# The gates of branches a and c of a two-layer encoder, computed first in each layer as seven products of quarters

## The chip, the cores and the metric

The kernel runs on one core of one Trainium2 chip. The metric is the device time in microseconds (us); lower is better. TensorE (PE) does the matrix products, VectorE (DVE) and ScalarE (ACT) the element work, GpSimd (POOL) little. DMAs are issued from the queues of SyncE (SP) and ACT. [...]

## The reference

Two layers over 640 tokens (512 of a prompt, 8 x 16 of samples), 1024 features, all in fp32. Three branches read the same normalised input, and each is scaled by a gate of its own:

```python
u = rms_norm(x, norm1_g)
z = u @ w_in
(xa, ga, mq, mk, mv, mo, mi, mf, aq, ak, av, g_a, g_b, g_c) = split(z)
...
y_a = (h_a * gelu(ga)) @ w_oa            # h_a: conv and linear recurrence (LRU) on xa
y_b = (h_m * sigmoid(mo)) @ w_ob         # h_m: mLSTM on mq, mk, mv, mi, mf, 4 heads
y_c = attention(q_c, k_all, v_all) @ w_oc  # window of 128, 16 heads, sinks
mix = sigmoid(g_a + b0) * y_a + sigmoid(g_b + b1) * y_b + sigmoid(g_c + b2) * y_c
x = x + mix @ w_out
x = x + square(relu(rms_norm(x, norm2_g) @ w_up)) @ w_down
```

Each of g_a, g_b, g_c is a product of 640 x 1024 by 1024 x 1024.

## The kernel before

**Products.** An fp32 product is made of three passes over pairs "hi" and "lo" of a shorter format: hi x hi, lo x hi, hi x lo. Weights come in blocks of 256 columns; the list `jobs` sets their order. For each block `prep` issues two DMAs of 512 KB on SP's queue (`wraw`, 2 buffers); ACT casts the hi part (`parts`, L164), DVE subtracts for the lo part (L166), into `whi` and `wlo` (6 buffers each). `gemm_w` takes a block as 96 matmuls of 128x320 (L293: two halves of columns, 8 steps of 128 rows, three passes, two halves of the tokens) into the two-buffered PSUM tile `acc`. `gemm_x` (L311) makes the transposed form. `strassen_w` (L255) takes a block as seven products of 12 matmuls, 84 in all, on quarter sums of weights (DVE, `wsum`, L186) and of input; before the change only the MLP's up projection uses it, and its `wsum` tiles come from the pool that `sums[0]` names.

**Order of a layer.** Norm of the input (`take_x`, `norm_scale`: the reciprocal root is a chain of small DVE operations, L120 to L125, at whose end the row `rbc` is spread by PE, L392, and copied); LRU; attention; mLSTM; merges; output projection; MLP. Plain products are dropped in between:

- `gate(i)` (L1010) is one block of branch i's gate: 96 matmuls, then per half a DVE multiplication by `rbc` (L1015), a tanh on ACT (L1016) and a store to the memory buffer `gdr[i]`. For branch a (i = 0) the result stays in SBUF (`kept`).
- `branch_a(j)` (L1023) is `gate(0)` followed by a block of `w_oa`, whose evacuation (L1029) multiplies with the kept gate. One stands in the attention, three after it.
- The attention works on 8 pairs of heads. A pair is: scores (L847), DVE maxima, exponentials on ACT (L825, L826), normalisation on DVE (L827 to L830), transposes on PE (L869), copies `pT`, products with the values (L877), and the transposes of the next pair's q (L969, L971), from which ACT and DVE make `qp`. After four pairs a sample group follows (L901, L915, L927, L937).
- The mLSTM works head by head: projections, four chunks and a last one (L672, L679, L682, L686), for which the 8 sample states pass through `cb` (L589 to L599, loads and stores of 256 KB each), the end of the head (`fin`, `num`, L715), transposes (L721).
- The four `gate(2)` stand behind the last head in the program, with the reload of the attention's output (`ydr[1]`) between them; the merges of c and b follow.

**What sets the order on an engine.** The program is written in the order above; a scheduler then orders each engine's list from a model of its own. It moves independent matmuls forward into gaps that its model sees, so a product that stands behind the attention in the program may fill the attention's pauses on PE. Such matmuls are called fillers below.

Of the kernel before, what the change touches and what calls it, by code (L numbers as in the profile page):

```python
# [9 lines left out]
F32 = mybir.dt.float32  # L10
F32R = mybir.dt.float32r
I32 = mybir.dt.int32
AF = mybir.ActivationFunctionType
# [8 lines left out]
NT = SEQ + DB * DS  # L22
# [53 lines left out]
def trunk(ctx: ExitStack, tc: tile.TileContext, I, O):  # L76
# [59 lines left out]
    def act_tile(p=None):  # L136
        return (p or actp).tile([128, 2, NT], F32R, name="at", tag="at")
# [179 lines left out]
    for l in range(depth):  # L317
        win = I["w_in"][l]

        def cols(c, n=256):  # L320
            return (win[:, c:c + n], n)

        seq = [[cols(c + 256 * h) for c in (C_MK, C_MQ, C_MV, C_MO)] for h in range(4)]
        ga = [cols(C_G[0] + 256 * j) for j in range(4)]
        gb = [cols(C_G[1] + 256 * j) for j in range(4)]
        gc = [cols(C_G[2] + 256 * j) for j in range(4)]
        oa, ob, oc, ow = [[(I[nm][l][:, 256 * j:256 * j + 256], 256) for j in range(4)] for nm in ("w_oa", "w_ob", "w_oc", "w_out")]
        for k, j in LRU_ORDER:
# [78 lines left out]
        return cv, cvh  # L407

    cv, cvh = vectors(0)
    xpool = tc.tile_pool(name="xp0", bufs=8)  # L410
    xp = xpool.__enter__()
    with tc.tile_pool(name="ld", bufs=1) as ld:
        xin = ld.tile([128, 5, D], F32, name="xin")
        xss = ld.tile([128, 10], F32, name="xss")
        xpr = I["x_prompt"][0].rearrange("(t p) d -> p t d", p=128)

        def load(h):
            c = slice(512 * h, 512 * h + 512)
            sp.dma_start(xin[:, 0:2, c], xpr[:, 0:2, c])
            sp.dma_start(xin[:, 2:4, c], xpr[:, 2:4, c])  # L420
            sp.dma_start(xin[:, 4, c], I["x_sample"].rearrange("b s d -> (b s) d")[:, c])

        load(0)
        for _ in prep(0, 0):
            pass
        load(1)
        for _ in prep(0, 1):
            pass
        prepared[0] = 1
        sp.dma_start(cs[:, 128:NCST], cst[:, 128:NCST])  # L430
        xs, u = [], []
        for m in range(8):
            x = xp.tile([128, NT], F32, name="x", tag="x")
            ps = ps_small()
            for t in range(4):
                pe.transpose(ps[:, 128 * t:128 * t + 128], xin[:, t, 128 * m:128 * m + 128], ident)
            dve.tensor_copy(x[:, 0:512], ps)
            ps = ps_small()
            pe.transpose(ps[:, 0:128], xin[:, 4, 128 * m:128 * m + 128], ident)
            act.copy(x[:, 512:640], ps[:, 0:128])  # L440
            xs.append(x)
            u.append(act_tile())
            split(u[m], x, cv[:, 8 * V_N1 + m:8 * V_N1 + m + 1])
            if m % 4 == 1:
                h = m // 4
                for t in range(5):
                    xsq = ld.tile([128, 512], F32, name="xsq", tag="xsq", bufs=2)
                    act.activation(xsq, xin[:, t, 512 * h:512 * h + 512], AF.Square, accum_out=xss[:, 5 * h + t:5 * h + t + 1])
        dve.tensor_tensor(vv[:, 0:5], xss[:, 0:5], xss[:, 5:10], ALU.add)


    def mlstm_gates(l, gp, gtp):
# [286 lines left out]
    def attention(l, ap):  # L739
# [206 lines left out]
        for j in range(4):  # L946
# [9 lines left out]
            if j == 0:  # L956
                gate(1)
            if j == 3:
                branch_a(0)
            gemm_x(u, ev_q, 264 if j == 0 else 256)  # L960
            if j == 1:
                gate(1)
# [21 lines left out]
    for l in range(depth):  # L984
# [18 lines left out]
        xpool.__exit__(None, None, None)  # L1003
        if l > 0:
            hdpool.__exit__(None, None, None)

        ngate = [0, 0, 0]
        kept = []

        def gate(i, keep=False):  # L1010
            def evac(m, acc):
                k = ngate[i]
                ngate[i] += 1
                sg = tr.tile([128, NT], F32, name="sg", tag="sg")
                dve.tensor_tensor(halves(sg), acc[:, :, 0:320], halves(rbc), ALU.mult)  # L1015
                act.activation(sg, sg, AF.Tanh, bias=half(V_BG + i, k), scale=0.5)  # L1016
                if keep:
                    kept.append(sg)
                else:
                    act.dma_start(gdr[i][128 * k:128 * k + 128, :], sg)  # L1020
            gemm_w(u, evac)

        def branch_a(j):  # L1023

            gate(0, True)

            def evac(m, acc):
                sg = kept.pop(0)
                dve.scalar_tensor_tensor(halves(sg), halves(sg), 1.0, acc[:, :, 0:320], op0=ALU.add, op1=ALU.mult)  # L1029
                k = 2 * j + m  # L1030
                sp.dma_start(mdr[128 * k:128 * k + 128, :], sg)
            gemm_w(hg, evac)

# [171 lines left out]


        gate(1)
        gate(1)
        with tc.tile_pool(name="at", bufs=1, reuse_waits="tile") as ap:
            attention(l, ap)  # L1210

# [7 lines left out]
        for j in range(1, 4):  # L1219
            branch_a(j)  # L1220
            if j == 1:
                mlstm_gates(l, gp, gtp)
        hgpool.__exit__(None, None, None)


# [14 lines left out]
        xpool = tc.tile_pool(name=f"xp{l + 1}", bufs=8, reuse_waits="tile")  # L1240
# [224 lines left out]
```

## Time and profile before

| what | value |
|---|---|
| time, median of 3 runs | 2901.86 us (2899.88 to 2904.1) |
| profiled execution, its own time | 2899.9 us |
| its span | 2898.1 us |
| mean granted clock of PE | 0.995 |
| PE busy | 2839.4 us (98%) |
| DVE busy | 1853.8 us (64%) |
| ACT busy | 1312.4 us (45%) |
| DMA | 319.5 MB, 110 GB/s over the span |

The profiled execution lies 2 us under the median; 1.8 us of its time are outside the span. "Busy" is the time in which at least one instruction of the engine ran. Matmuls overlap in the records, so a row of n matmuls that follows densely on another costs the distance between starts, which is a little under its stated duration.

### The profile page before, as it was taken

What the parts mean: (1) busy time and instruction counts of PE and PEld (TensorE: products, weight loads), DVE (VectorE), ACT (ScalarE), POOL (GpSimd) and SP (SyncE); (2) the same over time, 40 slices, a digit from 0 to 9 for tenths busy, and PEclk for the clock granted to TensorE, in tenths of its full rate; (3) what the DMA queues carried; (4) which work ended last, traced back from release to release, by engine and by line L of the source; (5) the groups of instructions that cost most, each with busy time, mean ns of one, the idle gap of its engine ahead of it and who ended that gap; (6) DMA issues with size and microseconds to landing.
All of it is one profiled execution on the core that took longest, in us unless ns stands there. A gap on an engine that the chain in (4) does not pass through costs nothing. (4 is left out here: it accounts for less than half of the span.)

```text
span 2898.1 us, 50789 instructions
## 1 busy us (share of the span) xinstructions
PE 2839.4 (98%) x20134; PEld 2799.9 (97%) x20134; DVE 1853.8 (64%) x3758; ACT 1312.4 (45%) x2767; POOL 26.7 (1%) x65
## 2 busy tenths in 40 slices
PE   8999999999999999999999999999999999999999
PEld 8999999999999999999999999999999999999999
DVE  7967566444565677676679676655445646667772
ACT  5764444333442445444357544443444324443452
POOL 0000000000000000000000000000000000000000
PEclk9999999999999999999999999999999999999999
DMA  5242224444573322222322322334445733222222
GB/s 174 65 123 81 76 82 123 120 136 138 158 259 125 104 72 81 81 80 81 113 67 79 116 73 84 96 101 147 131 141 152 264 110 102 74 88 73 80 81 81
DMA packets 276878, 319.53 MB, mean 110 GB/s; under 512 B 26424, under 2 KB 231016, under 8 KB 276608
## 3 DMA queue, kind: packets, MB, share of 16 engines
q1 hardware_dynamic: 267104, 300.03, 33.8%
q10 hardware_dynamic: 9536, 16.26, 1.6%
q8 instruction: 158, 2.59, 0.4%
q14 instruction: 80, 0.66, 0.1%
HBM read 255.76 MB, written 62.04 MB: 110 GB/s over the span
## 5 line engine op out<-in xcount | busy, mean ns | idle before, releaser
L293 PE MATMUL acc<-at,whi 128*128 128x320 f32 x5120 | 818.0, 312 | 6.9 <-ACT at L133 2.8
L293 PEld LDWEIGHTS acc<-at,whi 128*128 128x128 f32 x5120 | 765.3, 189 | 10.2 <-ACT at L133 3.4
L164 ACT CAST whi<-wraw 128x512 fp32r<-128x512 f32 x680 | 406.9, 619 | 512.7 <-PE acc L293 186.9
L166 DVE TENSOR_TENSOR wlo<-wraw,whi 128x512 fp32r<-128x512 f32 x680 | 451.3, 693 | 173.7 <-ACT whi L164 113.5
L311 PE MATMUL acc<-whi,at 128*128 128x256 f32 (+1 forms) x3040 | 408.5, 284 | 16.9 <-DVE qT L626 4.5
L293 PE MATMUL acc<-at,wlo 128*128 128x320 f32 x2560 | 415.6, 310 | 0.0
L311 PEld LDWEIGHTS acc<-whi,at 128*128 128x128 f32 x3040 | 378.2, 188 | 22.1 <-DVE qT L626 5.5
L293 PEld LDWEIGHTS acc<-at,wlo 128*128 128x128 f32 x2560 | 384.1, 188 | 0.7
L255 PE MATMUL acc<-at,whi 128*128 128x320 f32 x1536 | 266.9, 314 | 8.4 <-ACT at L130 5.5
L255 PEld LDWEIGHTS acc<-at,whi 128*128 128x128 f32 x1536 | 236.9, 191 | 14.4 <-ACT at L130 6.1
L311 PE MATMUL acc<-wlo,at 128*128 128x256 f32 (+1 forms) x1520 | 218.6, 282 | 0.2 <-DVE wlo L166 0.2
L311 PEld LDWEIGHTS acc<-wlo,at 128*128 128x128 f32 x1520 | 196.4, 188 | 0.6 <-DVE wlo L166 0.5
L277 PE MATMUL psb<-at,whi 128*128 128x320 f32 x896 | 171.1, 309 | 0.0
L277 PE MATMUL acc<-at,whi 128*128 128x320 f32 x896 | 169.0, 309 | 0.0
L255 PE MATMUL acc<-at,wlo 128*128 128x320 f32 x768 | 143.8, 310 | 0.0
L277 PEld LDWEIGHTS psb<-at,whi 128*128 128x128 f32 x896 | 141.6, 188 | 0.0
L277 PEld LDWEIGHTS acc<-at,whi 128*128 128x128 f32 x896 | 140.9, 188 | 0.0
L164 ACT CAST whi<-wsum 128x512 fp32r<-128x512 f32 x128 | 79.0, 619 | 129.1 <-PE acc L277 93.3
L255 PEld LDWEIGHTS acc<-at,wlo 128*128 128x128 f32 x768 | 121.5, 190 | 0.0
L166 DVE TENSOR_TENSOR wlo<-wsum,whi 128x512 fp32r<-128x512 f32 x128 | 87.8, 689 | 46.9 <-ACT whi L164 45.1
L277 PE MATMUL acc<-at,wlo 128*128 128x320 f32 x448 | 101.8, 308 | 0.0
L277 PE MATMUL psb<-at,wlo 128*128 128x320 f32 x448 | 100.6, 308 | 0.0
(372 smaller groups left out, 3613.1 us busy)
## 6 DMA issues: line engine op xcount, KB each, us to landing
wraw<-in_w_in SPq DMA_DIRECT2D x160, 512.0 KB
wraw<-in_w_up SPq DMA_DIRECT2D x64, 512.0 KB
wraw<-in_w_down SPq DMA_DIRECT2D x64, 512.0 KB
cb<-in_state_mlstm_C SPq DMA_DIRECT2D x64, 256.0 KB
out_C_s<-cb SPq DMA_DIRECT2D x64, 256.0 KB
gdr<-sg ACTq DMA_DIRECT2D x32, 320.0 KB
rl<-ydr SPq DMA_DIRECT2D x32, 320.0 KB
sg<-gdr SPq DMA_DIRECT2D x32, 320.0 KB
```

The source lines that it names most:

```text
L164: act.copy(hi if shape else hi[:, :, :src.shape[-1]], src)
L166: dve.tensor_tensor(lo if shape else lo[:, :, :src.shape[-1]], src, h.bitcast(F32), ALU.subtract)
L255: pe.matmul(bank[nm], ws[i][:, k, :], xs(nm, k)[:, part], start=(first and i == 0 and k == 0 and part == 0), stop=(i == 1 and k == 3), ski ...
L277: pe.matmul(o[s], lhs, hs[k][:, part, 320 * s:320 * s + 320], start=(k == 0 and i == 0 and part == 0), stop=(i == 1 and k == 3))
L293: pe.matmul(acc[:, s, 0:320], lhs, xs[k][:, part, 320 * s:320 * s + 320], start=(i == 0 and k == 0 and part == 0), stop=(i == 1 and k == 7),)
L311: pe.matmul(o, xs[k][:, part, 128 * t:128 * t + 128], wt[:, k % KQ, 0:n], start=(i == 0 and k == 0 and part == 0), stop=(i == 1 and k == 7),)
```

## The change

At the head of each layer, right behind the norm, two blocks of b's gate and then a new function, `strassen_gates`, make all of a's and c's gates: for four i, quarter sums of the scaled input rows i and 4 + i (two ACT copies, four DVE subtractions of 320 columns, two splits), then eight blocks by `strassen_w`, whose evacuations add the products, multiply by `rbc`, take the tanh and store to `gdr`. The LRU stands behind that. `branch_a` makes the `w_oa` product alone and loads its gate from `gdr[0]`. One block of b's gate stays behind the LRU, one in the attention. No gate is left behind the mLSTM.

```diff
+        jobs += [gb[0], gb[1]]
+        jobs += [(a, n, "s") for a, n in ga + gc]
         for k, j in LRU_ORDER:
             jobs.append(cols((C_XA, C_GA)[k] + 256 * j))
-        jobs += [gb[0], gb[1], cols(C_AKV), gb[2]]
+        jobs += [gb[2], cols(C_AKV), gb[3]]
         for j in range(4):
             if j == 3:
-                jobs += [ga[0], oa[0]]
+                jobs.append(oa[1])
             jobs.append(cols(C_AQ - 8, 264) if j == 0 else cols(C_AQ + 256 * j))
             if j == 1:
-                jobs.append(gb[3])
-        for j in range(1, 4):
-            jobs += [ga[j], oa[j]]
+                jobs.append(oa[0])
+        jobs += oa[2:]
         for j in range(4):
             jobs += seq[j]
-        jobs += gc + oc + ob
+        jobs += oc + ob
...
+    def strassen_gates(l, ut, u, xs, vec, half):
+        t12, t34, xg = [], [], {}
+        for i in range(4):
+            for k in (i, 4 + i):
+                xg[k] = ut.tile([128, NT], F32, name="xg", tag="xg", bufs=2)
+                act.activation(xg[k], xs[k], AF.Copy, scale=vec(V_N1, k))
+            a, b = xg[i], xg[4 + i]
+            t = ut.tile([128, NT], F32, name="ut12", tag="ut12", bufs=1)
+            dve.tensor_tensor(t[:, 0:320], a[:, 320:640], a[:, 0:320], ALU.subtract)
+            dve.tensor_tensor(t[:, 320:640], b[:, 320:640], t[:, 0:320], ALU.subtract)
+            t12.append(act_tile(ut))
+            split(t12[i], t)
...
+            def epi(nm, b):
+                if nm == "p1":
+                    kept["p1"] = copy("g1", b["p1"])
...
+                elif nm == "p6":
+                    u2 = copy("g2", b["p6"])
+                    dve.tensor_tensor(sg[0][:, 320:640], u2, b["p3"], ALU.add)
+                    dve.tensor_tensor(sg[0], sg[0], rbc, ALU.mult)
+                    done(0)
...
+        for i, j in [(0, j) for j in range(4)] + [(2, j) for j in range(4)]:
+            product = job(i, j)
...
+        with tc.tile_pool(name="ut", bufs=8, reuse_waits="tile") as ut:
+            sums[0] = ut
+            gate(1)
+            gate(1)
+            strassen_gates(l, ut, u, xs, vec, half)
...
         def branch_a(j):
 
-            gate(0, True)
-
             def evac(m, acc):
-                sg = kept.pop(0)
+                k = 2 * j + m
+                sg = tr.tile([128, NT], F32, name="sg", tag="sg")
+                with tc.issue_after(wlast[0].ins):
+                    sp.dma_start(sg, gdr[0][128 * k:128 * k + 128, :])
                 dve.scalar_tensor_tensor(halves(sg), halves(sg), 1.0, acc[:, :, 0:320], op0=ALU.add, op1=ALU.mult)
...
         yc = []
-        for j, n in enumerate((4, 0, 3, 0)):
-            yc += reload(ydr[1], hdp, range(len(yc), len(yc) + n))
-            gate(2)
-        yc += reload(ydr[1], hdp, range(7, 8))
+        yc += reload(ydr[1], hdp)
```

**PE in the second half of the attention.** Before, one pair of layer 0 (from its first scores) reads on PE's list; L293 are the fillers, L847, L869 and L877 the pair itself:

```order
L847 MATMUL psb<-kh_2338,qp_2362 128x192 x12
L293 MATMUL acc<-at,whi 128x320 x13
L293 MATMUL acc<-at,wlo 128x320 x16
L293 MATMUL acc<-at,whi 128x320 x14
L869 MATMUL psb<-cs,prob_2368 128x128 x2
L293 MATMUL acc<-at,whi 128x320
L869 MATMUL psb<-cs,prob_2369 128x128 x4
L293 MATMUL acc<-at,whi 128x320 x11
L869 MATMUL psb<-cs,prob_2370 128x128 x4
```

In the changed program the same pair reads as follows (the lines have moved: L920 are the scores, L942 the transposes, L950 the products with the values, L1042 and L1044 the next pair's q):

```order
L920 MATMUL psb<-kh_3684,qp_3708 128x192 x12
L942 MATMUL psb<-cs,prob_3714 128x128 x2
L942 MATMUL psb<-cs,prob_3715 128x128 x4
L950 MATMUL psb<-pT,vd 128x256
L942 MATMUL psb<-cs,prob_3716 128x128 x4
L942 MATMUL psb<-cs,prob_3717 128x128 x4
L950 MATMUL psb<-pT,vd 128x256 x2
L1042 MATMUL psb<-cs,q 128x128 x4
L950 MATMUL psb<-pT,vd 128x256 x4
L1044 MATMUL psb<-cs,q 128x128
L920 MATMUL psb<-kh_3684,qp_3707 128x64 x2
```

No filler is left: from the scores of pair 4 to the end of the second sample group PE's list holds 424 L293 and 48 L311 of other products before, and none of either in the changed program, in each of the two layers. All four `w_oa` blocks stand ahead of pair 4 there.

**PE in the last mLSTM head.** Before, from one chunk's last product to the next chunk (L293 are blocks of c's gate):

```order
L686 MATMUL psb<-vt,kw 128x257 x2
L672 MATMUL psb<-qT,kT 128x128 x2
L293 MATMUL acc<-at,whi 128x320 x22
L293 MATMUL acc<-at,wlo 128x320 x2
L679 MATMUL psb<-vt,pt 128x257
```

Changed (L759, L745, L752 and L755 are these same lines, moved):

```order
L759 MATMUL psb<-vt,kw 128x257 x2
L745 MATMUL psb<-qT,kT 128x128 x2
L752 MATMUL psb<-vt,pt 128x257
L755 MATMUL psb<-cp,qs 128x257 x2
L759 MATMUL psb<-vt,kw 128x257 x2
```

From the first chunk's product L679 (now L752) to the small transposes at the end of the mLSTM (L729, L734; now L802, L807) the list held 337 L293; 32 are left, and those belong to the first block of `w_oc`. Heads 0 to 2 and the attention's first half keep as many fillers as before, give or take a block.

**DVE at the head of layer 1.** The piece of the changed list that leads to the first evacuation of a product (L1086, b's gate); L461 to L467 are subtractions of quarter sums, L131 their splits, L186 sums of weights, L123 to L125 the reciprocal root:

```order
L131 TENSOR_TENSOR at<-ut_16711,at 128x640
L166 TENSOR_TENSOR wlo<-wsum,whi 128x512
L186 TENSOR_TENSOR wsum<-wraw,wsum 128x512
L124 SCALAR_TENSOR_TENSOR tt<-tt,vv 128x5
L131 TENSOR_TENSOR at<-ut_16717,at 128x640
L461 TENSOR_TENSOR ut_16727<-xg 128x320
L186 TENSOR_TENSOR wsum<-wraw 128x512
L125 SCALAR_TENSOR_TENSOR rtok<-tt,rtok 128x5
```

Before, the same steps of the root stand among small operations of the LRU and splits of weights:

```order
L123 TENSOR_TENSOR tt<-rtok 128x5
L1076 SCALAR_TENSOR_TENSOR sm<-sm 128x8
L166 TENSOR_TENSOR wlo<-wraw,whi 128x2x256
L1135 TENSOR_TENSOR lwl<-lwr,lwh 128x256
L124 SCALAR_TENSOR_TENSOR tt<-tt,vv 128x5
L166 TENSOR_TENSOR wlo<-wraw,whi 128x2x256
L1076 SCALAR_TENSOR_TENSOR sm<-sm 128x8
L125 SCALAR_TENSOR_TENSOR rtok<-tt,rtok 128x5
```

All four i of the quarter sums stand ahead of the first evacuation in layer 1 (16 subtractions and 8 splits), in layer 0 two and a half of the four.

## Rows read from the trace of the kernel before

**Rows 1.** The page, engines: busy us (share), instructions.
```profile
PE 2839.4 (98%) x20134; PEld 2799.9 (97%) x20134; DVE 1853.8 (64%) x3758; ACT 1312.4 (45%) x2767; POOL 26.7 (1%) x65
```

**Rows 2.** Windows, layer 0: stretch, length, busy (instructions) per engine, PEclk, DMA.
```profile
850.00:900.00 50.00, 50.00 (x343) 50.00 (x342) 27.44 (x39) 13.17 (x21) 0.00 (x0) 1.00 0.66 230
1050.00:1100.00 50.00, 50.00 (x344) 50.00 (x343) 35.46 (x60) 21.69 (x38) 0.00 (x0) 1.00 0.25 75
```

**Rows 3.** Groups by line and shape, DVE: count | busy us, mean ns | idle before.
```profile
L166 DVE TENSOR_TENSOR wlo<-wraw,whi 128x512 fp32r<-128x512 f32 x672 | 446.1, 693 | 168.7 <-ACT whi L164 113.5 <-PE acc L293 24.3 <-PE acc L255 8.1
L131 DVE TENSOR_TENSOR at<-rl,at 128x640 fp32r<-128x640 f32 x32 | 25.8, 823 | 27.1 <-ACT at L130 27.0
L1386 DVE TENSOR_TENSOR dn<-acc,rbc 128x320 f32<-128x320 f32 x112 | 49.5, 484 | 45.6 <-PE acc L277 45.5
L186 DVE TENSOR_TENSOR wsum<-wraw 128x512 f32<-128x512 f32 x64 | 44.2, 691 | 25.2 <-DMA wraw<-in_w_up 24.5
```

**Rows 4.** Windows of two stretches of layer 0, all engines.
```profile
370.00:471.50 101.50, 101.28 (x724) 98.96 (x723) 64.76 (x140) 44.89 (x139) 6.67 (x11) 1.00 0.30 92
772.30:844.60 72.30, 72.30 (x492) 71.15 (x491) 41.15 (x101) 29.39 (x63) 0.00 (x0) 1.00 0.54 174
```

**Rows 5.** The same two stretches, PE and PEld of L293 alone, then L311.
```profile
370.00:471.50 101.50, 68.31 (x409) 60.67 (x407) 1.00 0.30 92
772.30:844.60 72.30, 59.84 (x378) 55.73 (x377) 1.00 0.54 174
...
370.00:471.50 101.50, 6.06 (x48) 5.82 (x48) 1.00 0.30 92
```

**Rows 6.** Timeline, PE: scores of pairs 5 and 6 (start us, us, engine, line).
```profile
397.18 1.93 PE L847 MATMUL psb<-kh,qp 128*128 128x64 f32 x16
416.69 1.93 PE L847 MATMUL psb<-kh,qp 128*128 128x64 f32 x16
```

**Rows 7.** Timeline, DVE and ACT, within pair 5.
```profile
404.36 1.03 DVE L830 TENSOR_TENSOR prob<-prob,ssm 128x384 f32<-128x384 f32 x2
...
411.11 0.59 ACT L975 ACTIVATE qp<-psb 64x512 fp32r<-64x512 f32 x1 [2.14 <-PE psb L969]
...
413.38 0.69 DVE L976 SCALAR_TENSOR_TENSOR qp<-psb,qp 64x512 fp32r<-64x512 f32 x1 [0.24 <-ACT qp L975]
```

**Rows 8.** Timeline, PE: the second sample group, from its last scores to its end.
```profile
458.36 1.14 PE L915 MATMUL psb<-kcT,qsm 128*128 128x144 f32 x8
464.57 1.03 PE L927 MATMUL psb<-cs,sprob 128*128 128x128 f32 x8
471.41 0.39 PE L937 MATMUL psb<-pT,vn 128*128 128x128 f32 x2
```

**Rows 9.** Timeline, PE and DVE: chunks, sample states and end of head 3.
```profile
777.62 0.59 PE L679 MATMUL psb<-vt,pt 128*128 128x257 f32 x2
795.89 0.59 PE L679 MATMUL psb<-vt,pt 128*128 128x257 f32 x2
...
780.65 0.28 DVE L675 TENSOR_TENSOR pt<-psb,dmat 128x128 f32<-128x128 f32 x1
822.04 0.15 DVE L699 TENSOR_TENSOR den<-csum,psb 128x1 f32<-128x1 f32 x1
829.50 2.07 DVE L715 SCALAR_TENSOR_TENSOR num<-num,fin,mo 128x256 f32<-128x256 f32 x5
```

**Rows 10.** Timeline, PE, layer 0 near 1016 us: around a pause in the Strassen products.
```profile
1016.24 0.63 PE L255 MATMUL acc<-at,whi 128*128 128x320 f32 x1 [2.80 <-ACT at L130]
1021.68 4.41 PE L255 MATMUL acc<-at,whi 128*128 128x320 f32 x16
1026.52 1.33 PE L255 MATMUL acc<-at,whi 128*128 128x320 f32 x8
```

**Rows 11.** A window behind that pause: columns as in Rows 2.
```profile
1020.00:1024.00 4.00, 4.00 (x16) 3.96 (x17) 3.27 (x16) 1.04 (x2) 0.00 (x0) 0.50 0.00 0
```

**Rows 12.** Timeline, PE: the head of layer 1.
```profile
1473.22 6.40 PE L293 MATMUL acc<-at,whi 128*128 128x320 f32 x32 [1.61 <-DVE xq L1106]
```

More of the change, by code (lines that the diff above doesn't have):

```diff
@@ L409, in trunk @@
     cv, cvh = vectors(0)
-    xpool = tc.tile_pool(name="xp0", bufs=8)
+    xpool = tc.tile_pool(name="xp0", bufs=8, side="right")
     xp = xpool.__enter__()
@@ L449, in trunk, with operand, job, copy @@
         dve.tensor_tensor(vv[:, 0:5], xss[:, 0:5], xss[:, 5:10], ALU.add)
+    def strassen_gates(l, ut, u, xs, vec, half):
[10 more added lines that the diff above has]
+            split(t12[i], t)
+            t_ = ut.tile([128, NT], F32, name="ut34", tag="ut34", bufs=1)
+            dve.tensor_tensor(t_[:, 0:320], b[:, 320:640], a[:, 320:640], ALU.subtract)
+            dve.tensor_tensor(t_[:, 320:640], b[:, 0:320], t[:, 320:640], ALU.subtract)
+            t34.append(act_tile(ut))
+            split(t34[i], t_)
+        def operand(nm, i):
+            t, c = {"p1": (u[i], 0), "p2": (u[4 + i], 0), "p3": (u[4 + i], 1),
+                    "p5": (t12[i], 0), "p6": (t12[i], 1), "p7": (t34[i], 0), "p4": (t34[i], 1)}[nm]
+            return t[:, :, 320 * c:320 * c + 320]
+        def job(i, j):
+            sg, kept = {}, {}
+            def copy(nm, src):
+                t = ut.tile([128, 320], F32, name=nm, tag=nm, bufs=2 if nm == "g5" else 1)
+                act.copy(t, src)
+                return t
+            def done(c):
+                k = 2 * j + c
+                act.activation(sg[c], sg[c], AF.Tanh, bias=half(V_BG + i, k), scale=0.5)
+                act.dma_start(gdr[i][128 * k:128 * k + 128, :], sg[c])
+            def epi(nm, b):
+                if nm == "p1":
+                    kept["p1"] = copy("g1", b["p1"])
+                elif nm == "p5":
+                    kept["p5"] = copy("g5", b["p5"])
+                elif nm == "p2":
+                    sg[0] = tr.tile([128, NT], F32, name="sg", tag="sg")
+                    dve.tensor_tensor(sg[0][:, 0:320], kept["p1"], b["p2"], ALU.add)
+                elif nm == "p6":
[3 more added lines that the diff above has]
+                    done(0)
+                elif nm == "p7":
+                    sg[1] = tr.tile([128, NT], F32, name="sg", tag="sg")
+                    dve.tensor_tensor(sg[1][:, 320:640], kept["p5"], b["p7"], ALU.add)
+                    dve.tensor_tensor(sg[1][:, 320:640], sg[1][:, 320:640], rbc[:, 320:640], ALU.mult)
+                elif nm == "p4":
+                    dve.tensor_tensor(sg[1][:, 0:320], b["p4"], rbc[:, 0:320], ALU.mult)
+                    done(1)
+            return strassen_w(operand, epi)
+        before = None
+        for i, j in [(0, j) for j in range(4)] + [(2, j) for j in range(4)]:
+            product = job(i, j)
+            for nm in ("p1", "p5", "q7", "p2", "p3", "q4", "p6"):
+                if nm[0] == "p":
+                    product(nm)
+                elif before is not None:
+                    before("p" + nm[1])
+            before = product
+        before("p7")
+        before("p4")
@@ L958, in attention @@
             if j == 3:
-                branch_a(0)
+                branch_a(1)
             gemm_x(u, ev_q, 264 if j == 0 else 256)
             if j == 1:
-                gate(1)
+                branch_a(0)
             qv = q.rearrange("p t (h d) -> p t h d", d=64)
@@ L1007, in trunk, with gate @@
         ngate = [0, 0, 0]
-        kept = []
-        def gate(i, keep=False):
+        def gate(i):
             def evac(m, acc):
@@ L1207, in trunk @@
         gate(1)
-        gate(1)
         with tc.tile_pool(name="at", bufs=1, reuse_waits="tile") as ap:
@@ L1218, in trunk @@
         gtp = gtpool.__enter__()
[L1219 to L1222, printed above, removed]
+        branch_a(2)
+        mlstm_gates(l, gp, gtp)
+        branch_a(3)
         hgpool.__exit__(None, None, None)
@@ L1232, in trunk @@
         yc = []
-        for j, n in enumerate((4, 0, 3, 0)):
-            yc += reload(ydr[1], hdp, range(len(yc), len(yc) + n))
-            gate(2)
-        yc += reload(ydr[1], hdp, range(7, 8))
+        yc += reload(ydr[1], hdp)
         mix = []
-        xpool = tc.tile_pool(name=f"xp{l + 1}", bufs=8, reuse_waits="tile")
+        xpool = tc.tile_pool(name=f"xp{l + 1}", bufs=8, reuse_waits="tile", side="right")
         xp = xpool.__enter__() if l < depth - 1 else ctx.enter_context(xpool)
```

8 lines of the change are left out of this document (2 added, 6 removed).

## The prediction

> **What bounds the kernel now.** I read the page's engine part first: PE is busy 98% of the span, DVE 64%, ACT 45% [rows 1]. The reader is to see that almost no time is left in which PE waits, so what a change is worth is either matmuls taken away or new waits on PE. The windows by stage give the price of a matmul: 342 of 128x320 in 50 us of plain products [rows 2], 146.2 ns each; the MLP's Strassen stage runs at the same pace (344 in 50 us) although DVE is busy 35 of the 50 us there. Then I looked at what keeps PE full in the stages that have chains of their own, and there the windows say something else than the page: in the attention's second half [rows 4] 409 of 724 matmuls are L293 and 48 are L311 [rows 5], products that have nothing to do with the attention. The last mLSTM head is the same, 378 of 492. Those two stretches are bound by PE only because of the fillers; under them lie chains through ACT and DVE.
>
> **The products that go.** A plain block is 96 matmuls, a Strassen block 84. Sixteen blocks change (a and c, four each, two layers): 192 matmuls x 146.2 ns = **-28.1 us**.
>
> **The Strassen stage itself.** DVE per block: 7 `wlo` and 4 `wsum` at 0.69, three additions and two multiplications on 320 columns at 0.48, one on 640 at 0.82 (by the row of the same width) [rows 3]: 7.6 + 2.4 + 0.8 = 10.8 us, against 84 x 146.2 ns = 12.3 us of PE. It fits, as it does in the MLP [rows 2]. I take nothing; if DVE paced it with some waits in between, a tenth of 12.3 us per block would be 20 us in all.
>
> **Gates through memory.** The sixteen stores and reloads of 320 KB per branch and layer lie beside products, and ACT and the queues have room (DMA share 0.25 to 0.66 of the engines in dense stages [rows 2]). The reload in `branch_a` stands on SP's queue behind the last weight load, and its reader is an evacuation that comes a block later. Nothing; if each of the 16 evacuations waited a us, 16 us.
>
> **The fillers that go.** The order of the changed program shows the second half of the attention without any filler, and the last head with 32. Apart from the 28.1 us the matmuls have not vanished; they are done earlier, at the head of the layer, where they cover nothing. What matters is how long the two stretches take when bare.
>
> *Attention, pairs 4 to 7 and sample group.* The fillers are 409 x 0.146 + 6 = 65.7 us of the 101.5 us, so the stretch's own PE work is 35.8 us [rows 4, 5]. A pair takes 19.5 us now [rows 6]. Its bare chain, from pair 5: scores at 397.18 to the end of normalisation at 405.39 [rows 6, 7]; an evacuation of another product stands in between on DVE, 0.8 by a row of its width [rows 3], so 7.2 with its wait. Then transposes and products 1.0 each (estimated by the scores' 1.93 for 16 matmuls), a copy `pT` 0.7 (as L976, which copies as much [rows 7]), and the two rounds of ACT and DVE for the next q, 411.11 to 414.07 [rows 7], 3.0: **12.9 us**. Sample group and last pair without the next q: 10 for the pair, 3.8 to the end of the scores, 5.1 from there to L927 and 7.1 for the rest [rows 8]: 26. Bare stretch 3 x 12.9 + 26 = 64.7 us, so PE would be idle 64.7 - 35.8 = **29 us** that it now spends on fillers.
>
> *Last head.* Own PE work: 72.3 - 378 x 0.146 = 17.0 us [rows 4, 5]; with the 32 `w_oc` matmuls that stay, 21.7. Bare chain: a chunk from L679 to the next `pt`, 777.62 to 780.93 [rows 9], 3.3 us, four of them 13.2 where it was 18.3 us for three; the sample states took 795.89 to 822.04, 26 us [rows 9]: bare, I choose 20, since two states are in work at a time (some 3 us each, estimated by six operations of 0.5 to 0.7, as the rows of such widths [rows 3]), which bounds it at 12 from below, and loads and stores through five buffers hold it up; the root and scale 822.04 to 829.50, 7.5, of which weight splits take a part, 5; `num` 2.1; the last block of the attention's output, whose buffer comes free only then, 5 for load and split. Sum 45.3, idle **24 us**.
>
> **The clock.** The granted clock is 0.995 in the mean, but it falls where PE pauses: after an idle time of 2.80 us at 1016 [rows 10] 16 matmuls took 4.41 us where 8 took 1.33 at full clock, and the window 1020 to 1024 shows 0.50 with PE busy all the time [rows 11]. [...] In a bare pair PE pauses some 5 us in the softmax (7.2 less the scores' 1.93), and works about half of the time; so I expect 0.5 over most of both stretches. The chain then grows by PE's own parts: per pair 3 us (half of the scores, transposes, products), so 15.9, tail 33, stretch 80.7, lost time **45 us**. Last head: four chunks at 5.2, states 23, rest as before: 55, lost **33 us**. And PE is back at full pace only in the row at 1026.52, 10 us behind the pause [rows 10], so each stretch leaves up to 3 us behind it; I take 2, four times, 8 us. [...]
>
> **Head of a layer.** Both `acc` buffers are full when the first evacuation needs `rbc`, so PE waits for DVE's root; it does already (1.61 us of idle at the end [rows 12]). In layer 1 eight subtractions (0.4 effective), four splits (0.74), four weight sums and one split (0.6) now stand within the root, less an estimated 4.5 us of splits and small operations that stood there before and go: +4.7. Before the root 8.3 us of such work delay the sum of squares, of which 4 us fall in DVE's slack: +4. So +9; layer 0 about +4. Sum **+13 us**; bounds 3 and 25.
>
> **Sum.** -28.1 + 2 x (45 + 33) + 8 + 13 = +149 on the execution's own 2899.9 us, which lies 2 us under the median: **3048 us**. Chance 0.55, own range 3005 to 3090.
>
> **Rivals.** *The clock stays full* in the stretches, because scores, transposes and products come often enough: -28.1 + 2 x (29 + 24) + 13 = +91, 2991 us. For it: PE still works some 55% of a bare stretch (35.8 of 64.7 us), and the one fall above [rows 10] came behind a pause in which it did nothing at all. Chance 0.2.
>
> *The stretches hardly shorten*, because other things than PE's fillers set the pace (buffers of PSUM, the loads of sample states, the order of DVE): then all fillers are lost, 65.7 and 50.6 us per layer, +217, 3117 us. Against it: the parts of a pair's chain add up to 12.9 us from their rows, against a period of 19.5 [rows 6]. With half of the shortening, about 3080. Chance 0.15.
>
> *DVE or the weight sums pace the Strassen stage*: +20 on top of any case. Chance 0.02 that it is the main cause.
>
> *Faster: the fillers covered nothing*, since the chain contracts to PE's own work when it is not interrupted. Then -28.1 + 13: 2885 us. It decides where the four bare stretches leave less than 4 us idle each. Against it: four softmaxes of some 5 us, in which PE has nothing of its own, are already 20 us of idle in one layer's attention. Chance 0.06.
>
> *No change*: gain and idle balance at those 4 us. Chance 0.02.
>
> **Range and signs.** Between 2975 and 3100 lie the likeliest case, the one with full clock and part of the slower one, and about 2 in 10 is left out. About 0.2% (6 us) can be told from no change here. Faster 0.06, same 0.02, slower 0.92.
>
> **What would show it.** In the changed profile: L255 with 1344 more matmuls and L293 with 1536 fewer; PE's idle time up from some 60 us (span less busy [rows 1]) to over 150, ended by ACT and DVE at L942, L950, L920 in the attention and at L666, L670 and L794 in the mLSTM; the distance between the scores of pairs 4 to 7 about 16 us instead of 19.5, and the stretch some 80 us instead of 101; in the windows of these stretches PEclk near 0.5; the Strassen stage at the layer's head with 340 matmuls per 50 us; the first gate evacuation of layer 1 some 9 us later against the norm. The clock is wrong if PEclk is 1.00 in pairs 4 to 7; the whole forecast is wrong if these pairs come 10 us apart or less.

## The result and the profile after

The changed kernel takes 3059.5 us (median of 4 runs, 3055.12 to 3059.93) against 2901.68 us before: a ratio of 1.0538 (95% interval 1.0525 to 1.0551), 5.4% slower. The forecast was 3048 us with 2975 to 3100 as its range.

The page of the changed kernel, engines and the clock by slices of the span (compare [rows 1]):

```profile
PE 2867.7 (94%) x19942; PEld 2809.7 (92%) x19942; DVE 1980.3 (65%) x3982; ACT 1381.2 (45%) x2895; POOL 26.8 (1%) x65
...
PEclk9999998899989999999989999989999899999999
```

PE has 192 instructions fewer and yet is busy 28 us longer and idle 189 us of a span of 3057.1 us, against 59 us before. Longer busy with fewer matmuls is already a sign of the clock, which is 0.967 in the mean against 0.995 before: four of its dips stand where the fillers are gone, one at the head of layer 1. In the kernel before, PE's longest wait in total for one line was this (us in total, times, longest):

```profile
PE acc L255 <- ACT at L130: 5.5, 2, 2.8
```

The six longest in the changed kernel:

```profile
PE psb L942 <- DVE prob L903: 34.4, 9, 7.7
PE acc L311 <- ACT vd L853: 17.3, 2, 8.7
PE psb L794 <- DVE num L788: 17.0, 5, 7.3
PE psb L393 <- DVE rtok L125: 12.8, 2, 11.9
PE psb L920 <- DVE qp L1049: 10.5, 7, 1.7
PE psb L666 <- ACT ch L662: 9.8, 9, 2.3
```

L942 and L920 are the attention, L794 and L666 the mLSTM (13.9 of the 17.0 us at L794 in the last heads), L393 the head of the layer: the places that the forecast named. L311 waiting for `vd` is not among them. It is the product behind the keys and values, between LRU and attention.

The same stages, by the first matmul of each in the timelines of both kernels (us, layer 0 / layer 1):

| from, to | before | after | difference, both layers |
|---|---|---|---|
| end of the layer ahead to first LRU product | 61.1 / 475.1 | 193.6 / 613.6 | +270.9 |
| LRU | 90.6 / 90.5 | 90.5 / 90.6 | 0 |
| LRU to pair 0 | 93.6 / 93.7 | 93.7 / 94.2 | +0.6 |
| pair 0 to pair 4 | 124.8 / 124.8 | 118.8 / 118.9 | -11.9 |
| pair 4 to the end of the sample group | 101.4 / 101.4 | 75.6 / 75.7 | -51.5 |
| from there to the last head's first chunk | 301.0 / 298.8 | 298.9 / 301.8 | +0.9 |
| last head to the small transposes | 66.2 / 66.2 | 46.2 / 47.0 | -39.2 |
| merges to the second norm | 189.3 / 189.8 | 184.2 / 183.9 | -11.0 |

(The first row of layer 1 contains the MLP of layer 0.) The head of the layers got 2 x 126.3 us of products (192 L293 and 672 L255 each at 0.146) and 18 us of waiting. Everywhere else 960 L293 a layer are gone, the 768 of a's and c's gates and the 192 of the two blocks of b that now stand at the head: 281 us in all. Those stages became only 112 us shorter: 169 us, six tenths of the work taken out, had covered waits. By place, with the L293 counted in the traces of both kernels (per layer, layer 0):

| stretch | fillers gone, us | shorter by, us | had covered, us |
|---|---|---|---|
| LRU to pair 0 | 96 L293: 14.0 | -0.1 | 14 |
| pair 0 to pair 4 | 73 L293 less 48 L311 that came: 5 | 5.9 | 0 |
| pair 4 to the end of the sample group | 407 L293 and 48 L311: 65.2 | 25.8 | 39.4 |
| last head | 308 L293: 45.0 | 20.0 | 25.0 |
| merges | 74 L293: 10.8 | 5.1 | 5.7 |

(An L293 is taken at 0.1462 us, an L311 at 0.118, since 24 of them took 2.84 us from 317.66 us on in the changed kernel. On PE's list I had counted 424 L293 in the third stretch; the trace has 407.)

The two bare stretches as windows (answers to [rows 4]; stretch, length, busy per engine with instructions, PEclk, DMA):

```profile
496.61:572.22 75.61, 48.39 (x267) 42.17 (x267) 48.91 (x119) 30.31 (x117) 6.60 (x11) 0.75 0.07 22
871.15:917.35 46.20, 30.52 (x142) 24.76 (x141) 30.74 (x82) 19.71 (x49) 0.00 (x0) 0.74 0.48 151
```

The mean of 0.75 is made of 37.57 us near 0.50 and the rest of the stretch at 1.00. In the timeline of pairs 4 to 6 (answers to [rows 6, 7]) it shows as matmuls of two lengths:

```profile
506.32 1.56 PE L942 MATMUL psb<-cs,prob 128*128 128x128 f32 x6 [7.69 <-DVE prob L903]
...
515.76 2.01 PE L920 MATMUL psb<-kh,qp 128*128 128x64 f32 x16 [1.72 <-DVE qp L1049]
521.04 1.55 PE L942 MATMUL psb<-cs,prob 128*128 128x128 f32 x6 [3.27 <-DVE prob L903]
...
523.24 1.85 PE L942 MATMUL psb<-cs,prob 128*128 128x128 f32 x8
...
529.95 2.08 PE L920 MATMUL psb<-kh,qp 128*128 128x64 f32 x16 [1.72 <-DVE qp L1049]
```

The scores of pair 5 took 2.01 us for 16 at a clock of 1.00, the eight transposes behind the pause 1.85 us at 0.55 in the mean. Eight of them took 1.03 us in pair 5 before, at 1.00:

```profile
407.69 1.03 PE L869 MATMUL psb<-cs,prob 128*128 128x128 f32 x8
```

Pair 5 is 14.2 us long, pair 6 13.9: 12.9 was the bare estimate, 15.9 the one with half the clock. Pair 4 took 19.2 us. PE waits 7.69 us there, because DVE works on another block of q (L841 to L845, 499.82 to 505.76) ahead of the pair's normalisation.

How much the clock can have cost is bounded by the windows in which it was low. There are five in this stretch, each at 0.50 or 0.51, and one in the last head (the first of the five, their sum, the last head's):

```profile
501.00:511.25 10.25, 4.93 (x19) 4.31 (x20) 8.57 (x16) 2.63 (x11) 0.95 (x1) 0.50 0.13 30
...
sum 37.57, PE 22.50 PEld 19.43 DVE 25.05 ACT 16.82 POOL 0.95; mean PE 4.50 PEld 3.89 DVE 5.01 ACT 3.36 POOL 0.19
...
893.54:917.35 23.81, 12.49 (x39) 9.08 (x40) 18.12 (x51) 9.31 (x23) 0.00 (x0) 0.50 0.52 164
```

PE was busy 22.50 us near 0.50 in the attention and 12.49 us in the last head. From the 0.50, and from eight transposes that took 1.91 us at it (pair 4) and 1.03 at 1.00, I estimate that this work would take about half at the full clock, so that the clock cost at most 11 of the 39.4 us lost there, and at most 6 of the 25. The rest, 28 and 19 us or more, is pauses.

### The profile page after: what moved, and what is told of

Same layout as the page of the kernel before. It is cut to its first block, busy times and chain, and to the rows that moved or that the text cites. A ratio compares the mean times of both kernels' runs of the same rounds, so it can differ in the third digit from the quotient of the medians.

```text
span 3057.1 us, 50989 instructions
## 1 busy us (share of the span) xinstructions
PE 2867.7 (94%) x19942; PEld 2809.7 (92%) x19942; DVE 1980.3 (65%) x3982; ACT 1381.2 (45%) x2895; POOL 26.8 (1%) x65
## 4 chain that ended last, share of the span: by engine, by line
PE 81%; DVE 7%; DMA 6%; ACT 4%; issue 2%; SPq 0%; POOL 0%; ACTq 0%; DVEq 0%; POOLq 0%
PE acc L293 24%; PE acc L255 16%; PE acc L311 15%; PE acc L277 6%; PE psb L277 6%; PE psb L255 3%; DMA out_C_s<-cb 2%; PE psb L950 2%; DMA cb<-in_state_mlstm_C 1%; PE psb L942 1%; DVE wlo L166 1%; DMA rl<-ydr 1%; PE psb L759 1%; PE psb L1223 1%; PE psb L755 1%
## 5 line engine op out<-in xcount | busy, mean ns | idle before, releaser
L293 PE MATMUL acc<-at,whi 128*128 128x320 f32 x4096 | 654.5, 314 | 19.6 <-DVE sg L1130 9.6
L164 ACT CAST whi<-wraw 128x512 fp32r<-128x512 f32 (+1 forms) x664 | 398.3, 620 | 559.7 <-PE acc L293 207.7
L293 PEld LDWEIGHTS acc<-at,whi 128*128 128x128 f32 x4096 | 617.8, 191 | 22.9 <-issue 15.4
L166 DVE TENSOR_TENSOR wlo<-wraw,whi 128x512 fp32r<-128x512 f32 (+1 forms) x664 | 439.3, 686 | 200.4 <-ACT whi L164 142.6
L311 PE MATMUL acc<-whi,at 128*128 128x256 f32 (+1 forms) x3040 | 417.5, 287 | 36.1 <-ACT vd L853 17.3
L311 PEld LDWEIGHTS acc<-whi,at 128*128 128x128 f32 x3040 | 385.3, 191 | 42.5 <-ACT vd L853 17.9
L255 PE MATMUL acc<-at,whi 128*128 128x320 f32 x2304 | 392.1, 311 | 9.3 <-ACT at L130 6.4
L255 PEld LDWEIGHTS acc<-at,whi 128*128 128x128 f32 x2304 | 350.8, 189 | 15.6 <-ACT at L130 6.9
L293 PE MATMUL acc<-at,wlo 128*128 128x320 f32 x2048 | 326.5, 309 | 0.0
L293 PEld LDWEIGHTS acc<-at,wlo 128*128 128x128 f32 x2048 | 306.1, 188 | 0.0
L311 PE MATMUL acc<-wlo,at 128*128 128x256 f32 (+1 forms) x1520 | 218.8, 283 | 0.0
L255 PE MATMUL acc<-at,wlo 128*128 128x320 f32 x1152 | 214.9, 309 | 0.0
L164 ACT CAST whi<-wsum 128x512 fp32r<-128x512 f32 x192 | 118.8, 620 | 181.1 <-PE acc L277 93.3
L311 PEld LDWEIGHTS acc<-wlo,at 128*128 128x128 f32 x1520 | 197.9, 190 | 0.1
L255 PEld LDWEIGHTS acc<-at,wlo 128*128 128x128 f32 x1152 | 181.1, 189 | 0.0
L166 DVE TENSOR_TENSOR wlo<-wsum,whi 128x512 fp32r<-128x512 f32 x192 | 131.5, 688 | 59.1 <-ACT whi L164 56.4
L277 PE MATMUL acc<-at,whi 128*128 128x320 f32 x896 | 168.7, 309 | 0.0
L277 PEld LDWEIGHTS acc<-at,whi 128*128 128x128 f32 x896 | 140.8, 188 | 0.0
L277 PE MATMUL acc<-at,wlo 128*128 128x320 f32 x448 | 101.8, 308 | 0.0
```

The lines of the kernel that those rows point to most:

```text
L164: act.copy(hi if shape else hi[:, :, :src.shape[-1]], src)
L166: dve.tensor_tensor(lo if shape else lo[:, :, :src.shape[-1]], src, h.bitcast(F32), ALU.subtract)
L255: pe.matmul(bank[nm], ws[i][:, k, :], xs(nm, k)[:, part], start=(first and i == 0 and k == 0 and part == 0), stop=(i == 1 and k == 3), ski ...
L277: pe.matmul(o[s], lhs, hs[k][:, part, 320 * s:320 * s + 320], start=(k == 0 and i == 0 and part == 0), stop=(i == 1 and k == 3))
L293: pe.matmul(acc[:, s, 0:320], lhs, xs[k][:, part, 320 * s:320 * s + 320], start=(i == 0 and k == 0 and part == 0), stop=(i == 1 and k == 7),)
L311: pe.matmul(o, xs[k][:, part, 128 * t:128 * t + 128], wt[:, k % KQ, 0:n], start=(i == 0 and k == 0 and part == 0), stop=(i == 1 and k == 7),)
```

## The experiments

Two theories were set against each other. **Lost cover**: the plain gates had filled waits of PE, and the new place at the head of the layer has nothing to fill. **A cost of the new stage**: DVE, the weight sums or the trips through memory make each Strassen block dear, wherever the plain ones had been.

**Strassen or place.** The same places with plain products, no quarter sums:

```diff
-        jobs += [(a, n, "s") for a, n in ga + gc]
+        jobs += ga + gc
...
-            strassen_gates(l, ut, u, xs, vec, half)
+            for i in (0, 2):
+                for j in range(4):
+                    gate(i)
```

> The same places and the same trips through memory, but a's and c's gates are plain products (96 matmuls a block instead of 84) and there are no quarter sums. Theory (the place costs the time, the Strassen form itself saves): 28 us more for the matmuls less 12 to 18 us for the quicker head of a layer: 3070 to 3076 us, attention and last head as in the changed kernel. Rival (the Strassen stage costs more than it saves, by DVE or weight sums): 3059 us or less.

Measured 3072.05 us (ratio to before 1.0581, 1.0555 to 1.0607), in the expected window, and its stretches are 76.0 and 46.7 us long in layer 0, as bare as in the changed kernel. By the stages the two heads are 11.3 us longer: 28.1 us more of products, less 16.8 of the 18 us of waiting. So the Strassen form does save; the place costs. The Strassen products themselves run as densely as plain ones, as this window of the changed kernel shows:

```profile
50.00:100.00 50.00, 50.00 (x344) 50.00 (x343) 39.44 (x68) 26.14 (x47) 0.00 (x0) 1.00 0.39 113
```

**Memory.** The kernel before, with a's gates stored and loaded back:

```diff
-            gate(0, True)
+            gate(0)
...
-                sg = kept.pop(0)
+                sg = tr.tile([128, NT], F32, name="sg", tag="sg")
+                with tc.issue_after(wlast[0].ins):
+                    sp.dma_start(sg, gdr[0][128 * k:128 * k + 128, :])
```

> The kernel before with one part of the change alone: the gates of a are stored to memory and loaded back where they are used, instead of being kept in SBUF; all products plain and in their old places. Theory (memory is hidden): 2902 us within 5. Rival (the trip through memory holds up evacuations, 1 us each or more): 2910 us or more.

Measured 2901.62 us, ratio 0.9997 (0.9988 to 1.0006): the trip through memory is hidden.

**Each half back.** c's gates behind the last head again, or a's into the attention again, the other four blocks staying at the head (the edit for c, in part):

```diff
-        jobs += [(a, n, "s") for a, n in ga + gc]
+        jobs += [(a, n, "s") for a, n in ga]
...
-        jobs += oc + ob
+        jobs += gc + oc + ob
...
+            gate(2)
```

> The gates of c go back behind the last mLSTM head as plain products; only a's four blocks per layer stay in the Strassen stage at the head of the layer. Theory (lost cover): the last head was idle about 25 us per layer without fillers, and the four blocks lose 7.0 us of saving: 3059.5 - 49 + 14 = about 3024 us, with the stretch from the head's first chunk to its end back at 66 us and PEclk 1.00 there; the attention's second half stays at 76 us. Rival (the Strassen stage itself, its DVE work and its trips through memory cost the time, so much a block): half the blocks, half the loss, about 2980 us.

> The mirror image: a's gates go back into the attention and behind it as plain products kept in SBUF; c's four blocks stay at the head as Strassen products. Theory (lost cover): the attention's second half was idle or slow for about 40 us per layer, so 3059.5 - 80 + 14 = about 2993 us, the stretch back at 101 us with PEclk 1.00, the last head still at 46 us; where the additional block also covers the wait for the keys and values ahead of the attention (8.7 us per layer) up to 25 us less. Rival (a cost per Strassen block): the same time as with c back, about 2980 us.

Measured 3012.92 us for c back (1.0381, 1.0351 to 1.0411) and 3005.71 us for a back (1.0357, 1.0326 to 1.0387). Neither is near the rival's 2980, but each is some 12 us off the theory's forecast, and they lie closer together than I expected. By the stages of layer 0: with c back the head of the layer is 48.6 us shorter (four blocks of 12.3), the last head 21.0 longer and the merges 5.3. 56.1 us of plain products thus cost 26.3: they cover **30 us** a layer, more than the 25 of the expectation, which had not counted the merges. With a back, 56.1 us of products cost about 22 us: they cover **34 us**, fewer than the 40. The second half of the attention was not full again in that run:

```profile
453.35:547.27 93.92, 87.75 (x602) 83.65 (x600) 59.55 (x132) 39.25 (x132) 6.60 (x11) 0.96 0.27 85
```

It holds 285 L293 there, before it was 407; the rest of a's products stand in the first half.

**Work moved to where cover is missing.** Two of b's plain blocks go behind the last head, one from the head of the layer and one from the start of the attention; the work stays the same:

> Both a and c stay Strassen products at the head; two of b's plain gate blocks (one from the head, one from the start of the attention) move behind the last mLSTM head, where they can fill it. The work is the same, only the place changes. Theory (lost cover): the last head's 25 us per layer are filled, 3059.5 - 49 = about 3010 us; up to 28 us more if the block taken from the start of the attention is missed there. Rival (Strassen stage, DVE or memory cost the time): no change, 3055 to 3065 us.

Measured 3061.77 us: nothing gained, a clear miss. The last head's window in this run (layer 0):

```profile
854.33:921.36 67.03, 54.20 (x332) 51.68 (x331) 38.12 (x94) 28.21 (x61) 0.00 (x0) 0.87 0.53 167
```

67.0 us is as long as with all four blocks of c back (67.2 us with 451 matmuls), with 332 matmuls and pauses in it. The timelines tell where fillers cover and where they don't (layer 0, us, with the number of L293 in brackets; "two behind" is this run, "held" the next one):

| part of the last head | before | changed | two behind | held |
|---|---|---|---|---|
| chunks (first to last L752) | 23.5 (95) | 13.5 (8) | 23.5 (95) | 13.0 (0) |
| sample states (to the last L666 or L670) | 27.3 (145) | 21.0 (16) | 29.9 (119) | 29.1 (143) |
| end of the head, transposes | 15.4 (96) | 11.7 (4) | 13.7 (4) | 15.6 (86) |

Between the chunks 87 fillers more, 12.7 us, cost 10.0: the scheduler has put 24 behind each chunk, while the chunk's chain leaves PE well under a microsecond, as the changed kernel shows:

```profile
873.59 0.70 PE L752 MATMUL psb<-vt,pt 128*128 128x257 f32 x2 [0.53 <-DVE pt L748]
877.16 0.67 PE L752 MATMUL psb<-vt,pt 128*128 128x257 f32 x2 [0.69 <-DVE pt L748]
```

They delay the chain by four fifths of their length. In the sample states of the kernel before, 129 fillers more, 18.9 us, cost 6.3. I had read them as nearly free (22.5 us with them), because I took the last L593, at 818.35 us, for the end; the last product with a state was L597, 4.9 us later (the second row is of the run with two blocks behind):

```profile
823.21 0.29 PE L597 MATMUL psb<-kvs 128*128 128x258 f32 x1
907.05 1.01 PE L670 MATMUL psb<-kvs 128*128 128x258 f32 x4
```

Taking them as nearly free, I held the two blocks behind the first product with a sample state:

```diff
             yc += reload(ydr[1], hdp, range(len(yc), len(yc) + n))
-            gate(1)
+            with tc.issue_after(smark[0].ins):
+                gate(1)
```

> As the run with two of b's gate blocks behind the last head, but these two blocks are ordered behind the first product with a sample state, so that none can stand between the chunks. Theory (a filler costs nothing only where the stage's own chain is waiting; between chunks 94 of them cost 10 us, in the sample states they were nearly free): the last head takes about 50 us instead of 67, 3061.8 - 34 = about 3028 us. Rival (fillers delay the sample states and the end of the head just as much): 3052 to 3062 us.

Measured 3046.29 us (1.0492, 1.0469 to 1.0515), 15 us less than the run before it: the direction is that of lost cover, the size less than half. The last head took 57.7 and 56.0 us instead of 67.0 and 68.8. The chunks were bare again, at 13.0 us, but the sample states stayed at 29.1, far from the 21.0 that "nearly free" had meant. The merges took 6 us more: 3.4 of them are 23 matmuls of `w_oc` that no longer stood in the head, and the rest stays open.

**Fillers held back in the attention.** Three `w_oa` blocks ordered behind the scores of pairs 4, 5 and 6:

```diff
-        branch_a(2)
-        mlstm_gates(l, gp, gtp)
-        branch_a(3)
+        for j in (1, 2, 3):
+            with tc.issue_after(marks[HOLDAT[j - 1]].ins):
+                branch_a(j)
...
```

> As the changed kernel, but three of the four w_oa blocks are ordered behind the scores of pairs 4, 5 and 6, so that the scheduler can't use them up earlier: 288 fillers (42 us) in the attention's second half, as many fewer in its first. Theory (lost cover): the second half takes about 80 us instead of 76 and its clock stays at 1.00, the first half gets shorter by up to 42 us as far as its own chain lets it: 2985 to 3025 us. Rival (the first half starves instead): nothing gained, 3055 to 3065 us, with PE idle between pairs 0 and 4.

Measured 3058.17 us: the rival. The windows of layer 0, pair 0 to 4 and pair 4 to the end:

```profile
379.20:478.05 98.85, 74.38 (x538) 69.47 (x537) 67.42 (x154) 44.34 (x144) 1.91 (x2) 0.90 0.19 62
478.05:571.49 93.44, 89.66 (x603) 86.42 (x603) 59.81 (x137) 37.56 (x129) 6.61 (x11) 0.94 0.29 95
```

48 us of products (288 L293, 48 L311) went from the first half to the second. The first half gave up 20 us, the second took 18. The first had not been over-full: without these blocks PE is idle there for 24 us and the clock falls to 0.90. The whole attention is short of products, and moving those that are left did not mend it.

**The clock.** Useless short matmuls in the pause of the softmax, 48 a pair:

```diff
+                if pair >= 4 and H == 1:
+                    for i in range(48):
+                        pe.matmul(pss[i % 2][:, 192:256], q[:, i % 8].rearrange("p a d -> p (a d)"), kh[g][:, 0, 0:64],
+                                  start=True, stop=True)
```

> As the changed kernel, with 48 extra matmuls of 64 columns in each of pairs 4 to 7, whose results are used nowhere: 17 stand ahead of the last four scores, 29 in PE's pause of the softmax, 2 behind the first transposes. They add about 3 us of work a pair in the pause and nothing useful. Theory (the pause drops the clock to half, and the pair's transposes and products then take twice as long): PEclk 0.9 or more in pairs 5 to 7, eight transposes 1.0 us instead of 1.9, the pairs 12.5 to 13.2 us apart instead of 14.0, the total down by 4 to 10 us, 3050 to 3055 us. Rival (the extra work only delays the chain, or the clock is no part of the loss): pairs 14 us or more apart, 3058 us or more.

Measured 3066.56 us (1.0565, 1.0547 to 1.0582), 7 us more than the changed kernel: the rival's time. It doesn't answer the question, because the clock came back only in part, although PE was busy nearly all the time. The stretch from pair 4 to the end of the sample group in this run:

```profile
496.71:576.62 79.91, 72.80 (x458) 64.65 (x459) 47.27 (x119) 30.70 (x117) 6.60 (x11) 0.83 0.07 21
```

The clock is 0.83 in the mean instead of 0.75. Pair 4 became 2.0 us shorter, but pairs 5 and 6 took 15.9 and 16.8 us instead of 14.2 and 13.9: work of no use put into PE's pause lengthened their chain. How much of the stretch's loss is the clock's is therefore not measured; the bound of 11 us above stands.

**The head of the layer.** DVE's subtractions and splits of quarter sums behind the copy of `rbc`:

```diff
+            held = tc.issue_after(rbcmark[0].ins)
+            held.__enter__()
             t = ut.tile([128, NT], F32, name="ut12", tag="ut12", bufs=1)
...
             split(t34[i], t_)
+            held.__exit__(None, None, None)
```

> As the changed kernel, but DVE's subtractions and splits of the input's quarter sums are ordered behind the copy of rbc, so that the first evacuations of a layer don't wait for them. Theory (the head of a layer waits for DVE's root, which stands behind the quarter sums: 18 us over both layers by the stretches from norm to norm): 12 us less, 3044 to 3051 us, PE's longest wait for rtok down from 11.9 us to about 2. Rival (the wait only moves to the first Strassen products, which need those sums): 3055 to 3062 us.

Measured 3045.12 us (1.0489, 1.0470 to 1.0509), 14.4 us less than the changed kernel. PE at the head of layer 1, first the changed kernel:

```profile
1552.58 2.50 PE L393 MATMUL psb<-cs,rtok 128*128 128x128 f32 x10 [11.87 <-DVE rtok L125]
1556.49 7.67 PE L293 MATMUL acc<-at,whi 128*128 128x320 f32 x32 [1.40 <-DVE sg L1086]
```

then the run with the sums held:

```profile
1540.79 1.38 PE L394 MATMUL psb<-cs,rtok 128*128 128x128 f32 x10 [1.67 <-DVE rtok L125]
1546.33 5.97 PE L293 MATMUL acc<-at,whi 128*128 128x320 f32 x26 [4.16 <-DVE sg L1090]
```

The 11.87 us went down to 1.67, and the wait behind it rose to 4.16, but the first Strassen products did not wait for the sums, since two plain blocks stand ahead of them. By the stages the heads of the layers became 1.1 and 9.1 us shorter; the rest lies in stages that the edit doesn't touch.

**The stretch that the forecast left out.** One block of b's gate from the head back to behind the LRU, so that two stand ahead of the keys and values as before:

```diff
-        jobs += [gb[2], cols(C_AKV), gb[3]]
+        jobs += [gb[1], gb[2], cols(C_AKV), gb[3]]
...
```

> As the changed kernel, with one of the two plain blocks of b's gate moved from the head of the layer to behind the LRU, so that two stand there before the keys and values, as before the change. Theory (the stretch from the LRU to pair 0 took 94 us both with and without this block, so it lost 14 us of cover per layer that the prediction did not count): 3059.5 - 28 = about 3031 us, the stretch still 94 us, PE's wait for vd of 8.7 us mostly gone. Rival (other waits of the stretch stay, the block only lengthens it): 3045 to 3060 us.

Measured 3032.08 us (1.0446, 1.0425 to 1.0466), 27 us less; by the stages 23 of them lie in the heads of the layers. The stretch from the LRU to pair 0 stayed at 93.7 us, and the wait for `vd` is gone from the list of waits. In the changed kernel it reads, with the window around it:

```profile
313.13 3.74 PE L311 MATMUL acc<-whi,at 128*128 128x256 f32 x16 [8.67 <-ACT vd L853]
...
300.00:316.00 16.00, 7.33 (x38) 7.06 (x39) 10.19 (x20) 6.34 (x13) 3.29 (x5) 0.61 0.48 154
```

A block of 14.0 us had been wholly covered here; taking it out freed nothing, and the clock fell as well (16 matmuls of 128x256 took 3.74 us there, at 0.50, and 2.05 at 317.66, at 1.00).

**Three repairs at once**, c's gates back, the sums held, the block of b back:

> Three repairs of the changed kernel together: c's gates back behind the last head (alone -47 us), the quarter sums behind the copy of rbc (alone -14), one block of b's gate back from the head to behind the LRU (alone -27). What is left of the change are a's four Strassen blocks at the head and the bare second half of the attention. Theory (four separate places, whose losses add): 3059.5 - 47 - 14 - 27 = 2971 us, within 8, and of the 70 us left above the time before nearly all in the stretch from pair 4 to the sample group's end and at the layer's head. Rival (the losses overlap, one place's wait stands in for another's): 2985 us or more.

Measured 2993.09 us (1.0315, 1.0297 to 1.0332): between the two, on the rival's side of the line. PE's longest waits in this run say why:

```profile
PE psb L946 <- DVE prob L907: 33.2, 9, 7.7
PE acc L255 <- ACT at L130: 16.7, 8, 3.3
PE psb L924 <- DVE qp L1053: 10.5, 7, 1.7
```

L255 waits for the splits of the quarter sums: 16.7 us, where the changed kernel has 6.4 at this line. The second plain block at the head, which went back behind the LRU, had been the cover of the held sums. Two repairs had used one and the same block. By the stages this makes some 14 of the 17 us that the profiled execution (2988.19 us) lies over the theory's forecast, in the heads of the layers; the rest stays open. No version that I ran is faster than the kernel before.

## Why the prediction was right, and where not

The direction and the mechanism were right, and the total was near: 3048 forecast, 3059.5 measured. That it came so near is in part luck, because a term that was left out (29 us) stood against two that were too large (some 24). By its steps:

- **Products that go**, -28.1 us: right within what can be seen. With plain products at the same place the heads grew by 11.3 us, which is 28.1 less the 16.8 us of waiting that fell away with the quarter sums.
- **Strassen stage and memory**, nothing each: right. Windows in the stage (50 to 150 us) have 344 and 343 matmuls in 50 us, at 39 us of DVE; the memory trip alone made 0.9997.
- **Attention**, 45 us a layer: a little large, 39.4 by the fillers that went and the time that they left behind. The stretch took 75.6 us instead of the forecast 80.7. Inside it two errors met: pair 4 took 19.2 us, since its chain holds DVE's work on q that pair 5, from which I had built all pairs, doesn't have; pairs 5 and 6 took 14.2 and 13.9 us and not 15.9, the tail 28.3 and not 33. The clock was 0.75 in the mean and not near 0.5.
- **Last head**, 33 us: 25 in the stretch and 5.7 behind it in the merges, 30 by the run with c's gates back. The forecast's 55 us hold 5 us for the last block of the attention's output, and that wait came behind the 46.2 us of the table's row, for an evacuation that stands behind the block's reload and split on DVE's list:

```profile
927.87 6.38 PE L293 MATMUL acc<-at,whi 128*128 128x320 f32 x32 [4.81 <-DVE sg L1130]
```

  The sample states bare took 21.0 us, where I had chosen 20, 23 with the clock.
- **The clock**: too large. It had 16 of the attention's 45 us and 9 of the last head's 33; by the low windows it can have been 11 and 6 at most. The pauses, 29 and 24 in the forecast, were 28 and 19 or more. The 2 us that I put behind each stretch can't be seen behind the attention, where the next stage is as long as before (+0.9 us over both layers), and behind the last head they can't be told from the wait above.
- **Head of a layer**, +13: 18 by the stages, of which holding the sums took away 10. The order of DVE's list was enough to see it: in the trace DVE ran the piece of its list in the listed order, from L131 at 1545.12 us to L125 at 1548.87, and PE waited 11.87 us for the root. For the rates the forecast named no row; the starts there lie 0.40 us apart behind a subtraction, 0.74 behind a split and 0.60 behind a weight sum, as it had taken them.
- **The step that was missing**: I looked for fillers in two stretches and took for granted that the rest of the layer stayed as it was ("Heads 0 to 2 and the attention's first half keep as many fillers as before, give or take a block"). Between LRU and pair 0 one block fewer stood, and the cover that it had been was its full 14.0 us in each layer.

Of the rivals, the one with the clock always full (2991) falls by the granted clock of the stretches (0.75 and 0.74); that the stretches hardly shorten (3117) falls by 75.6 and 46.2 us; that the fillers covered nothing (2885) falls by the time itself and by the three runs that put plain blocks back where they had stood; that the Strassen stage is paced by DVE or the weight sums falls by its dense windows and by the run with plain products there. Behind the pauses of pairs 4 to 7 (7.69, 3.27, 3.20 and 2.94 us) eight transposes took 1.91, 1.85, 1.59 and 1.45 us, against 1.03 before; the last section has a fall behind 8.33 us in which PE was busy throughout. How the loss divides between pauses and clock is bounded above, not measured.

## What to carry to other kernels

A matmul that stands in another stage's pause is paid for only in part; before it is made cheaper somewhere else, measure how much longer the stage is with it than without: here 281 us of products had cost 112. Look for such cover in every stage, also in those that the change doesn't name, by comparing the order of the lists from one fixed point to the next. That a saving in matmuls belongs first into stages that have no chain of their own to hide follows from this, but no run here tested it.

## What the runs showed of the hardware

In one place the clock of PE fell without a pause. In the run with the useless matmuls PE was busy without a break from 513.07 us on, for 8.33 us at a clock of 1.00; 48 of its 73 matmuls there were the useless ones, of 64 columns. The next 3.40 us ran at 0.50, with PE busy all the time:

```profile
513.07:521.40 8.33, 8.33 (x73) 8.23 (x72) 3.94 (x13) 2.15 (x11) 0.00 (x0) 1.00 0.10 35
521.50:524.90 3.40, 3.40 (x10) 2.33 (x9) 1.66 (x4) 1.85 (x10) 0.00 (x0) 0.50 0.01 2
```

Over the whole stretch from pair 4 on, the clock was 0.83 with PE busy 72.80 of 79.91 us, and in the changed kernel 0.75 with PE busy 48.39 of 75.61. Busy time itself grew where the clock was low (eight transposes took 1.91 us at 0.50 and 1.03 at 1.00), so it is no measure of the work done here.
